# Scores in row groups, all weight splits on VectorE, a planner that knows of a shared port

## Chip, cores and metric

One core of a Trainium2 chip runs the whole program. The metric is the device time of one execution in microseconds (us), lower is better. Before the change three timed runs gave 1037.95, 1039.11 and 1043.07, median 1039.11.

## What is computed

A trunk of two layers on x of 256 positions by 1024 features, all in float32. Each layer is a SwiGLU feed-forward net (FFN), a mixer, and a second FFN, every one between two RMS norms:

```python
for l in range(2):
    h = rmsnorm(x, g[0]);  x = x + 0.5 * rmsnorm(swiglu(h, wg[l,0], wu[l,0], wd[l,0]), g[1])
    h = rmsnorm(x, g[2])
    m = even_mixer(h, ...) if l % 2 == 0 else odd_mixer(h, ...)
    x = x + rmsnorm(m, g[3])
    h = rmsnorm(x, g[4]);  x = x + 0.5 * rmsnorm(swiglu(h, wg[l,1], wu[l,1], wd[l,1]), g[5])
# even mixer, A: 4 heads, two softmaxes each, 64 wide:  w = p0 - lam * p1;  o = rmsnorm(w @ v, subln) * 0.8
# even mixer, B: 8 heads on the 64 keys that an indexer selects:
#     score = sum over 8 indexer heads of relu(qi . ki) * wi   (32 wide),  top-64 of it,  softmax
# odd mixer, C: 16 heads, 64 wide, a band with a relative-position bias
```

`swiglu(h) = (silu(h wg) * (h wu)) wd` with 2816 hidden features.

## The kernel before

**Products.** A float32 product is three TensorE products on rounded halves: hi x hi, lo x hi, hi x lo (`mm3`, L381, lines 383 to 385; `products`, L364, lines 375, 376, 378). Weights come by DMA on SP's queue into a `raw` tile (`Unit.start`, L245). ScalarE casts 512 columns to `wh` (L264), and `wl = raw - wh` follows (L266) on VectorE (DVE) or GpSimd (POOL). Of 664 such splits 33 run on POOL, all in the two mixers: 20 from 191 to 316 us and 13 from 709 to 820 us. Activations are split likewise when a PSUM bank is emptied (`split`, L346: hi by ScalarE in L351, lo by DVE in L357).

**Stages.** First FFN 0 to 190 us, even mixer to 340, two FFNs to 708, odd mixer to 840, last FFN. A norm ends a stage and begins the next: `postnorm` (L467) updates X (L487), `prenorm` (L418) squares, takes a root on POOL (`rstd`, L409, lines 411 to 415), multiplies by g (L430 or L440), transposes on TensorE (L393) and splits into `xTh`, `xTl`. Matmuls of the other half of the positions fill in.

**Attention.** `split_keys` (L658) writes the transposed keys into KB with one head of a pair in partitions 0 to 63 and the other in 64 to 127, each in its own columns, with zeros elsewhere (`zeros`, L315), in two ScalarE and two DVE instructions of 64 partitions. `scores` (L685) then does two heads at once in six 128-row matmuls with 256 (first 128 queries) or 512 columns. It is called 16 times: 4 A heads, 4 B pairs, 8 C pairs. `soft` (L701) adds the mask, takes the maximum and the exponential. An A head divides its first softmax by its sum (L865), scales the second's reciprocal by -lam (L861) and adds it (L869). `select` (L793) computes the indexer's scores: for each of two query tiles and four groups of 32 partitions six matmuls into a bank of its own, a relu, two DVE accumulations.

**Order.** Nothing is ordered by hand. `Plan.op` (L61) records each operation with its engines, a cost, its reads and writes and a due place; `Plan.issue` (L93) is a list scheduler that plays the program through with these costs (and `LAT`, L30, from the end of one to the start of a dependent one) and writes each engine's instructions in the order in which it started them. An engine on the chip keeps this order. A weight split of a mixer may go to POOL where DVE is late by more than `OVER` (L38). The few lines that do it:

```python
if fits and e != o["eng"][0] and eng[o["eng"][0]] < now + o["over"]:
    fits = False                                        # L133, the second engine waits its turn
...
op(DVE if pl.over is None else ("DVE", "POOL"), {"DVE": n_dve(self.step), "POOL": 0.11 + self.step * 0.00218}, lo, ...)
```

Of the kernel before, what the change touches and what calls it, by code (L numbers as in the profile page):

```python
# [9 lines left out]
F32 = mybir.dt.float32  # L10
# [27 lines left out]

OVER = (None, 0.45, 0.5)
# [13 lines left out]
class Plan:  # L53
# [39 lines left out]
    def issue(self):  # L93
# [3 lines left out]
        ev, n = [], 0  # L97
# [16 lines left out]
        while ev:  # L114
# [7 lines left out]
            for e in heap:  # L122
# [3 lines left out]
                while heap[e]:  # L126
# [6 lines left out]
                    if fits and e != o["eng"][0] and eng[o["eng"][0]] < now + o["over"]:  # L133
                        fits = False
# [17 lines left out]
                us = o["us"][e] if isinstance(o["us"], dict) else o["us"]  # L152
                o["fn"](e) if isinstance(o["us"], dict) else o["fn"]()
                end = eng[e] = o["end"] = now + us
# [28 lines left out]
def trunk_kernel(  # L183
# [52 lines left out]
    class Unit:  # L236
# [8 lines left out]
        def start(self, n):  # L245
# [13 lines left out]
            for i, p in enumerate(range(0, f, self.step)):  # L259
# [5 lines left out]
                def lo(e, sl=sl):  # L265
                    (nc.vector if e == "DVE" else nc.gpsimd).tensor_sub(  # L266
                        ref.t[1][:, sl], raw.t[:, sl], ref.t[0][:, sl].bitcast(F32))
                op(ACT, n_act(self.step), hi, r=[rk], w=[(ref, i, 0)], pos=q)
                op(DVE if pl.over is None else ("DVE", "POOL"), {"DVE": n_dve(self.step), "POOL": 0.11 + self.step * 0.00218}, lo,
                   r=[rk, (ref, i, 0)], w=[(ref, i, 1)], pos=q + 0.05)  # L270
# [42 lines left out]
    KB.t = tuple(cp.tile([P, 4, 2 * S], F32R, name="KB" + c) for c in "hl")  # L313

    def zeros():  # L315
        for z in KB.t:
            nc.gpsimd.memset(z[0:64, :, S:2 * S].bitcast(F32), 0.0)
            nc.gpsimd.memset(z[64:P, :, 0:S].bitcast(F32), 0.0)
# [19 lines left out]
    def more_consts(after):  # L338
# [3 lines left out]
        op(POOL, 3.6, zeros, w=[(KB, "z")], after=after, pos=60.0)  # L342
# [3 lines left out]
    def split(dst, wk, src, rk, n, scale=None, sk=(), psum=True, pos=None):  # L346
# [14 lines left out]
        op(ACT, n_act(n, psum, int(callable(scale))), hi, r=list(rk) + list(sk), w=wk[0], pos=pos)  # L361
        op(DVE, n_dve(n), lo, r=list(rk) + list(sk) + wk[0], w=wk[1], pos=pos)
# [46 lines left out]
    def rstd(s, ep, pos):  # L409
# [3 lines left out]
        op(POOL, 0.11, lambda: nc.gpsimd.tensor_add(s.t[:, 2:3], s.t[:, 2:3], s.t[:, 1:2]), r=[(s, 1)], w=[(s, 2)], pos=pos)  # L413
        def power():
            nc.gpsimd.tensor_tensor(s.t[:, 3:4], s.t[:, 2:3], nhalf.t[:, 0:1], op=ALU.pow)
        op(POOL, 0.46, power, r=[(s, 2), nhalf], w=[(s, 3)], pos=pos)

    def prenorm(t, xT, g):  # L418
# [48 lines left out]
    def postnorm(t, y, g, half, final):  # L467
# [16 lines left out]
        for h, c0, n in CUTS if final else [(h, 0, 512) for h in range(2)]:  # L484
# [4 lines left out]
            o = op(DVE, n_dve(n) + 0.06, up, r=[yg[h], (s, 3)], w=[(X[t], h)], pos=pos)  # L489
# [584 lines left out]
```

## Time and profile before

| | |
|---|---|
| runs | 1037.95, 1039.11, 1043.07 us |
| the profiled execution | 1040.63 us, span 1038.9, mean granted clock 0.995 |
| PE busy | 1012.1 us, 97% of the span |
| DVE, ACT, POOL busy | 664.6 (64%), 555.1 (53%), 94.6 (9%) |
| DMA | 185.46 MB, 179 GB/s |

The times of all views come from the one profiled execution. Its own time of 1040.63 us holds the span of 1038.9 and 1.7 us around it. Matmuls overlap in the trace (a 512-column matmul is shown as 0.39 us, and one starts every 0.23 us), so PE's cost is read from start to start. An idle time in brackets names the engine, tile and line that ended it.

### The profile page before, as it was taken

The page shows a single profiled execution, that of the slowest core. Times are in us where ns is not written, and L with a number is a line of the kernel's source. Part 1 is how long each engine was busy: PE and PEld are TensorE (multiplying, and loading weights), DVE is VectorE, ACT ScalarE, POOL GpSimd, SP SyncE. Part 2 cuts the span into 40 slices and gives each one's busy share as a digit, 9 for nine tenths or more (in the row PEclk, how much of TensorE's full clock was granted, in tenths as well). Part 3 has the DMA queues.
Part 4 walks back from the last instruction along what each step waited for, and adds up shares of the span by engine and source line. Part 5 has one row for each costly group of instructions (what it writes and reads, how often), then busy time and mean ns, then how long its engine had stood idle before and what let it go on. Part 6 is the DMA issues. An engine that isn't in the chain of part 4 may idle for free.

```text
span 1038.9 us, 14338 instructions
## 1 busy us (share of the span) xinstructions
PE 1012.1 (97%) x5070; PEld 850.1 (82%) x5070; DVE 664.6 (64%) x1278; ACT 555.1 (53%) x1142; POOL 94.6 (9%) x117
## 2 busy tenths in 40 slices
PE   8999999999999999999999999999989999999997
PEld 7888888776778988888888888887889888888886
DVE  6655555689998765555487545555677886555552
ACT  7544444555657654454366544544567766444541
POOL 2000000232431100000010000003121110000000
PEclk9999999999999999999999999998999999999999
DMA  8866665463244576665457656654594356656641
GB/s 267 289 184 183 196 186 166 136 213 104 83 162 124 175 255 190 188 184 194 150 203 229 194 183 184 191 194 120 173 278 145 118 164 205 199 183 184 190 133 41
DMA packets 94152, 185.46 MB, mean 179 GB/s; under 512 B 7040, under 2 KB 29440, under 8 KB 94080
## 3 DMA queue, kind: packets, MB, share of 16 engines
q1 hardware_dynamic: 94080, 184.54, 56.8%
q8 instruction: 40, 0.66, 0.3%
q14 instruction: 32, 0.26, 0.1%
HBM read 183.47 MB, written 1.05 MB: 178 GB/s over the span
## 4 chain that ended last, share of the span: by engine, by line
PE 83%; DVE 8%; DMA 4%; issue 2%; ACT 2%; POOL 1%; SPq 0%; POOLq 0%; DVEq 0%; ACTq 0%
PE ps L384 14%; PE ps L383 14%; PE ps L385 14%; PE y L383 9%; PE y L384 9%; PE y L385 9%; PE ps L393 4%; PE ps L375 3%; PE ps L376 3%; PE ps L378 3%; DVE wl L266 2%; ACT wh L264 1%; DMA raw<-in_ow_in_dram 1%; DMA raw<-in_wg_dram 1%; DMA raw<-in_wu_dram 1%
## 5 line engine op out<-in xcount | busy, mean ns | idle before, releaser
L266 DVE TENSOR_TENSOR wl<-raw,wh 128x512 fp32r<-128x512 f32 x631 | 421.4, 708 | 286.0 <-ACT wh L264 285.2
L264 ACT CAST wh<-raw 128x512 fp32r<-128x512 f32 (+1 forms) x664 | 378.1, 616 | 319.1 <-PE ps L385 173.4
L384 PE MATMUL ps<-wl,xTh 128*128 128x512 f32 x592 | 231.0, 390 | 0.0
L383 PE MATMUL ps<-wh,xTh 128*128 128x512 f32 x592 | 231.0, 390 | 0.0
L385 PE MATMUL ps<-wh,xTl 128*128 128x512 f32 x592 | 230.9, 390 | 0.0
L383 PE MATMUL y<-wh,blk 128*128 128x512 f32 x352 | 140.2, 398 | 0.0
L385 PE MATMUL y<-wh,blk 128*128 128x512 f32 x352 | 138.2, 393 | 0.0
L384 PE MATMUL y<-wl,blk 128*128 128x512 f32 x352 | 137.9, 392 | 0.0
L385 PEld LDWEIGHTS ps<-wh,xTl 128*128 128x128 f32 x592 | 111.5, 188 | 23.3
L383 PEld LDWEIGHTS ps<-wh,xTh 128*128 128x128 f32 x592 | 111.5, 188 | 23.2
L384 PEld LDWEIGHTS ps<-wl,xTh 128*128 128x128 f32 x592 | 111.4, 188 | 23.0
L375 PE MATMUL ps<-wh,xTh 128*128 128x512 f32 (+2 forms) x320 | 108.4, 354 | 0.9 <-ACT xTh L351 0.9
L376 PE MATMUL ps<-wl,xTh 128*128 128x512 f32 (+2 forms) x320 | 105.6, 346 | 0.2 <-DVE wl L266 0.2
L413 POOL TENSOR_TENSOR sm<-sm 128x1 f32<-128x1 f32 x24 | 9.8, 408 | 767.2 <-ACT t L476 714.9
L385 PEld LDWEIGHTS y<-wh,blk 128*128 128x128 f32 x352 | 66.6, 189 | 14.3
L383 PEld LDWEIGHTS y<-wh,blk 128*128 128x128 f32 x352 | 66.8, 190 | 13.2
L384 PEld LDWEIGHTS y<-wl,blk 128*128 128x128 f32 x352 | 66.8, 190 | 13.2
L393 PE MATMUL ps<-ident,t 128*128 128x128 f32 x386 | 58.8, 278 | 13.3 <-DVE t L546 2.9
L393 PEld LDWEIGHTS ps<-ident,t 128*128 128x128 f32 x386 | 44.6, 141 | 29.5 <-issue 5.9
L375 PEld LDWEIGHTS ps<-wh,xTh 128*128 128x128 f32 x320 | 61.0, 191 | 7.8 <-ACT xTh L351 1.1
L376 PEld LDWEIGHTS ps<-wl,xTh 128*128 128x128 f32 x320 | 60.9, 190 | 6.7 <-DVE wl L266 0.6
L378 PE MATMUL ps<-wh,xTl 128*128 128x512 f32 (+2 forms) x320 | 65.8, 344 | 0.0
(129 smaller groups left out, 1071.8 us busy)
## 6 DMA issues: line engine op xcount, KB each, us to landing
raw<-in_wu_dram SPq DMA_DIRECT2D x88, 512.0 KB, 4.3
raw<-in_wd_dram SPq DMA_DIRECT2D x88, 512.0 KB, 3.5
raw<-in_wg_dram SPq DMA_DIRECT2D x86, 512.0 KB, 3.7
raw<-in_ew_in_dram SPq DMA_DIRECT2D x24, 512.0 KB, 3.8
raw<-in_ow_in_dram SPq DMA_DIRECT2D x24, 512.0 KB, 4.8
g<-in_norm_g_dram SPq DMA_DIRECT2D x11, 512.0 KB, 5.3
raw<-in_ew_out_dram SPq DMA_DIRECT2D x8, 512.0 KB, 3.9
raw<-in_ow_out_dram SPq DMA_DIRECT2D x8, 512.0 KB, 3.6
```

What stands on the lines that cost most here:

```text
L264: nc.scalar.copy(ref.t[0][:, sl], raw.t[:, sl])
L266: (nc.vector if e == "DVE" else nc.gpsimd).tensor_sub(ref.t[1][:, sl], raw.t[:, sl], ref.t[0][:, sl].bitcast(F32))
L375: nc.tensor.matmul(o(), ah, bh, start=k == 0, stop=False)
L376: nc.tensor.matmul(o(), ah, bl, start=False, stop=False)
L378: nc.tensor.matmul(o(), al, bh, start=False, stop=k == KT - 1)
L383: nc.tensor.matmul(o, ah, bh, start=start, stop=False)
L384: nc.tensor.matmul(o, ah, bl, start=False, stop=False)
L385: nc.tensor.matmul(o, al, bh, start=False, stop=stop)
L393: nc.tensor.transpose(b.t[:, k * P:(k + 1) * P], s[:, k * P:(k + 1) * P], ident.t)
L413: op(POOL, 0.11, lambda: nc.gpsimd.tensor_add(s.t[:, 2:3], s.t[:, 2:3], s.t[:, 1:2]), r=[(s, 1)], w=[(s, 2)], pos=pos)
```

## The change

1. POOL does no weight split: all 664 are DVE's. `OVER` is gone.
2. The planner has a `port` flag: POOL's operations and DVE's with two inputs in SBUF play one after another. An operation for PE is ready `SAFE` = 0.6 us later than before. ScalarE's latency is 0.14 instead of 0.07, POOL's small operations of a norm cost 0.27 and 0.52 instead of 0.11 and 0.46, and a few others more.
3. KB has no zeros: its columns are halved, `split_keys` is one ScalarE and one DVE instruction of 128 partitions, and `zeros` is gone. `scores` gives each head a bank, and does twelve matmuls of 64-row groups, the two groups in turn.
4. `select` takes four banks at once and does its 24 matmuls of a query tile round the four 32-row groups in turn, in one visit for each tile.
5. The first softmax of an A head is not divided: the second is scaled by -lam r0/r1, and the squared sum r0² goes into the epsilon of the norm that follows.

```diff
-LAT = {"PE": 0.2, "ACT": 0.07, "DVE": 0.13, "POOL": 0.17, "DMA": 2.0}
+LAT = {"PE": 0.2, "ACT": 0.14, "DVE": 0.13, "POOL": 0.17, "DMA": 2.0}
+SAFE = 0.6
-OVER = (None, 0.45, 0.5)
...
-                end = eng[e] = o["end"] = now + us
+                start = now
+                if o["port"]:
+                    start = max(start, port)
+                    port = start + us
+                end = eng[e] = o["end"] = start + us
...
-                    d["ready"] = max(d["ready"], end + (OWN[e] if d["eng"] == (e,) else o["lat"]))
+                    d["ready"] = max(d["ready"], end + (OWN[e] if d["eng"] == (e,) else o["lat"] + (SAFE if d["eng"] == ("PE",) else 0.0)))
...
-                op(DVE if pl.over is None else ("DVE", "POOL"), {"DVE": n_dve(self.step), "POOL": 0.11 + self.step * 0.00218}, lo,
+                op(DVE, n_dve(self.step), lo, r=[rk, (ref, i, 0)], w=[(ref, i, 1)], pos=q + 0.05, port=True)
...
-    KB.t = tuple(cp.tile([P, 4, 2 * S], F32R, name="KB" + c) for c in "hl")
+    KB.t = tuple(cp.tile([P, 4, S], F32R, name="KB" + c) for c in "hl")
...
-        for r in range(2):
-            rs = slice(64 * r, 64 * r + 64)
-            split(lambda rs=rs, r=r: tuple(z[rs, b0:b0 + n, r * S + c0:r * S + c0 + w] for z in KB.t),
+        split(lambda: tuple(z[:, b0:b0 + n, c0:c0 + w] for z in KB.t),
...
             def f(t=t):
-                mm3(bs[t].t[:, 0:2 * KL[t]].rearrange("p (h c) -> p h c", h=2), tuple(z[:, bq, t * P:(t + 1) * P] for z in q()),
-                    tuple(z[:, bk, :].rearrange("p (h c) -> p h c", h=2)[:, :, 0:KL[t]] for z in KB.t), True, True)
-            op(PE, 0.327 * (t + 1), f, r=qk + kb_keys(bk), w=[bs[t]], pos=pos, after=after)
+                for i, j in ((0, 0), (0, 1), (1, 0)):
+                    for h in range(2):
+                        rs = slice(64 * h, 64 * h + 64)
+                        nc.tensor.matmul(bs[h].t[:, QS[t]], q()[i][rs, bq, t * P:(t + 1) * P], KB.t[j][rs, bk, 0:KL[t]],
+                                         start=i + j == 0, stop=i == 1)
+            op(PE, 0.36, f, r=qk + kb_keys(bk), w=[(b, t) for b in bs], pos=pos, after=after)
...
+            for i in range(2):
+                def f(i=i):
+                    for x, z in ((0, 0), (0, 1), (1, 0)):
+                        for g in range(4):
+                            rs = slice(32 * g, 32 * g + 32)
+                            nc.tensor.matmul(bs[g].t[:, i * kl:(i + 1) * kl], iT.v()[x][rs, i, t * P:(t + 1) * P],
+                                             iT.v()[z][rs, 2, 0:kl], start=x + z == 0, stop=x == 1)
+                op(PE, 0.36, f, r=ik, w=[(b, i) for b in bs])
...
-                nc.vector.reciprocal(ri.t, r.t)
-                nc.vector.tensor_scalar(ri.t[:, 2:4], ri.t[:, 2:4], nlam.t, None, op0=ALU.mult)
+                nc.vector.reciprocal(ri.t[:, 2:4], r.t[:, 2:4])
+                nc.vector.scalar_tensor_tensor(ri.t[:, 2:4], ri.t[:, 2:4], nlam.t, r.t[:, 0:2], op0=ALU.mult, op1=ALU.mult)
+                nc.vector.tensor_mul(rsq.t[:, :, h], r.t[:, 0:2], r.t[:, 0:2])
...
-                def nr(t=t, e=es[0], ri=ri):
-                    nc.vector.tensor_scalar(e.t[:, QS[t]], e.t[:, QS[t]], ri.t[:, t:t + 1], None, op0=ALU.mult)
```

**Where the order moves.** In the rows below a number behind a name counts the tiles, so the same tile has another number in the two kernels; the line of a matmul is 5 less in the changed kernel.

First place: PE's queue at the start, where the second half of x is transposed (`t_50`) between the first gate and up matmuls of the first FFN. Before:

```order
L383 MATMUL ps_380<-wh_261,xTh_130 128x512
L384 MATMUL ps_380<-wl_262,xTh_130 128x512
L385 MATMUL ps_380<-wh_261,xTl_131 128x512
L393 MATMUL ps_386<-ident,t_50_378 128x128 x2
L383 MATMUL ps_373<-wh_261,xTh_130 128x512
L384 MATMUL ps_373<-wl_262,xTh_130 128x512
```

And with the change:

```order
L378 MATMUL ps_376<-wh_259,xTh_131 128x512
L379 MATMUL ps_376<-wl_260,xTh_131 128x512
L380 MATMUL ps_376<-wh_259,xTl_132 128x512
L388 MATMUL ps_393<-ident,t_50_373 128x128 x2
L378 MATMUL ps_369<-wh_284,xTh_131 128x512
L379 MATMUL ps_369<-wl_285,xTh_131 128x512
```

The transposes stand behind 12 matmuls of the weight tile where they stood behind 6.

Second place: PE's queue where the second FFN pair ends (`y`, the down product) and the odd mixer begins (`xTh`, the normed and transposed x). Before:

```order
L385 MATMUL y_5382<-wh_6316,blk_6394 128x512
L393 MATMUL ps_6528<-ident,t_1180_6479 128x128 x4
L393 MATMUL ps_6536<-ident,t_1183_6491 128x128 x4
L383 MATMUL y_5377<-wh_6336,blk_6393 128x512
...
L385 MATMUL y_5382<-wh_6377,blk_6394 128x512
L375 MATMUL ps_6584<-wh_6468,xTh_6542 128x512
```

And with the change:

```order
L380 MATMUL y_5408<-wh_6389,blk_6430 128x512
L388 MATMUL ps_6572<-ident,t_1182_6517 128x128 x4
L388 MATMUL ps_6579<-ident,t_1183_6523 128x128 x4
L378 MATMUL y_5414<-wh_6389,blk_6430 128x512
...
L380 MATMUL y_5414<-wh_6410,blk_6431 128x512
L370 MATMUL ps_6612<-wh_6501,xTh_6588 128x512
```

Behind the eight transposes stood 18 matmuls of the down product (the "..." holds 16 of them), now 9 (7): the transposes come 9 matmuls later.

Third place: PE's queue at the first pair of the odd mixer's scores. `ps_6946` is the next Q projection. Before:

```order
L385 MATMUL ps_6946<-xTh_6542,wl_6777 128x256
L383 MATMUL ps_6990<-KBh,blk_6872 128x256
L384 MATMUL ps_6990<-KBl,blk_6872 128x256
L385 MATMUL ps_6990<-KBh,blk_6872 128x256
L383 MATMUL ps_6995<-KBh,blk_6872 128x512
L384 MATMUL ps_6995<-KBl,blk_6872 128x512
```

And with the change:

```order
L688 MATMUL ps_7016<-KBh,blk_6905 128x128
L688 MATMUL ps_7017<-KBh,blk_6905 128x128
L688 MATMUL ps_7016<-KBl,blk_6905 128x128
L688 MATMUL ps_7017<-KBl,blk_6905 128x128
...
L688 MATMUL ps_7016<-KBh,blk_6905 128x256
L688 MATMUL ps_7017<-KBh,blk_6905 128x256
```

Six matmuls are twelve with half the columns each, in two banks by turns; they stand behind as many Q matmuls as before.

## Rows read from the trace of the kernel before

**Rows 1.** The profile page's first part, the span's busy time, share and instructions by engine.

```profile
PE 1012.1 (97%) x5070; PEld 850.1 (82%) x5070; DVE 664.6 (64%) x1278; ACT 555.1 (53%) x1142; POOL 94.6 (9%) x117
```

**Rows 2.** Table by stretch: us of the span, its length, busy us (and instructions) of PE, PEld, DVE, ACT, POOL, granted clock, DMA share, GB/s. Four stretches of the even mixer, the boundary to the odd mixer, one stretch inside the odd mixer.

```profile
208.00:234.00 26.00, 25.42 (x133) 20.28 (x132) 23.26 (x46) 14.46 (x28) 10.49 (x12) 1.00 0.64 214
234.00:260.00 26.00, 23.86 (x118) 17.97 (x118) 24.31 (x65) 14.72 (x37) 6.73 (x5) 1.00 0.33 100
260.00:286.00 26.00, 23.89 (x130) 19.79 (x129) 25.83 (x82) 15.78 (x47) 11.60 (x8) 1.00 0.28 84
286.00:312.00 26.00, 23.86 (x118) 18.62 (x117) 23.95 (x55) 14.28 (x40) 9.52 (x8) 1.00 0.47 160
702.00:728.00 26.00, 23.42 (x94) 18.79 (x93) 16.16 (x24) 13.65 (x30) 8.78 (x10) 0.87 0.41 122
780.00:806.00 26.00, 26.00 (x204) 24.94 (x203) 21.06 (x65) 19.35 (x52) 5.38 (x7) 1.00 0.49 148
```

**Rows 3.** Groups of instructions from 208 to 312 us, DVE's and then POOL's: count, busy us, mean ns of one, idle before and what ended it.

```profile
L266 DVE TENSOR_TENSOR wl<-raw,wh 128x512 fp32r<-128x512 f32 x33 | 32.7, 1031 | 1.4 <-ACT wh L264 1.3
L357 DVE TENSOR_TENSOR KBl<-ps,KBh 64x512 fp32r<-64x512 f32 x8 | 5.5, 688 | 1.7 <-ACT KBh L351 1.6
L865 DVE TENSOR_SCALAR t<-t,sm 128x256 f32<-128x256 f32 x4 | 1.4, 348 | 0.0
L865 DVE TENSOR_SCALAR t<-t,sm 128x128 f32<-128x128 f32 x4 | 1.1, 277 | 0.0
L861 DVE TENSOR_SCALAR sm<-sm,nlam 128x2 f32<-128x2 f32 x4 | 0.9, 230 | 0.1
...
L266 POOL TENSOR_TENSOR wl<-raw,wh 128x512 fp32r<-128x512 f32 x15 | 21.5, 1449 | 33.7 <-ACT wh L264 33.7
L642 POOL TENSOR_TENSOR t<-t,t 128x512 f32<-128x512 f32 x8 | 11.8, 1469 | 14.5 <-DVE t L639 14.5
```

**Rows 4.** DVE's timeline: one weight split in the even mixer, four in the odd one where POOL does no large work. Start, us, engine, line, operation, count, idle before.

```profile
246.41 1.77 DVE L266 TENSOR_TENSOR wl<-raw,wh 128x512 fp32r<-128x512 f32 x1
...
742.13 2.50 DVE L266 TENSOR_TENSOR wl<-raw,wh 128x512 fp32r<-128x512 f32 x4 [3.55 <-ACT wh L264]
```

**Rows 5.** PE's timeline at the start of the program, the transposes of `t_50` and a matmul behind them.

```profile
23.50 0.39 PE L385 MATMUL ps<-wh,xTl 128*128 128x512 f32 x1
26.31 0.44 PE L393 MATMUL ps<-ident,t 128*128 128x128 f32 x2 [2.43 <-DVE t L546]
...
28.00 0.63 PE L385 MATMUL ps<-wh,xTl 128*128 128x512 f32 x1
```

**Rows 6.** The boundary to the even mixer: PE's transposes, DVE's product with g, POOL's weight splits.

```profile
194.28 0.66 PE L393 MATMUL ps<-ident,t 128*128 128x128 f32 x4 [0.87 <-DVE t L430]
195.50 0.66 PE L393 MATMUL ps<-ident,t 128*128 128x128 f32 x4 [0.56 <-DVE sm L411]
...
192.93 2.52 DVE L430 TENSOR_TENSOR t<-X,g 128x512 f32<-128x512 f32 x2
...
191.25 3.65 POOL L266 TENSOR_TENSOR wl<-raw,wh 128x296 fp32r<-128x296 f32 x3 [0.27 <-ACT wh L264]
```

**Rows 7.** The boundary to the odd mixer: DVE's scaling by the root and g (the first half of the positions, and the second, 18 us later), PE's transposes, two of the matmuls behind them.

```profile
714.19 3.43 DVE L440 SCALAR_TENSOR_TENSOR t<-X,sm,g 128x512 f32<-128x512 f32 x2 [0.44 <-POOL sm L415]
732.31 1.40 DVE L440 SCALAR_TENSOR_TENSOR t<-X,sm,g 128x512 f32<-128x512 f32 x2
...
716.00 0.66 PE L393 MATMUL ps<-ident,t 128*128 128x128 f32 x4 [1.56 <-DVE t L440]
717.67 1.11 PE L393 MATMUL ps<-ident,t 128*128 128x128 f32 x4 [1.02 <-DVE t L440]
719.44 0.63 PE L385 MATMUL y<-wh,blk 128*128 128x512 f32 x1
723.28 0.62 PE L385 MATMUL y<-wh,blk 128*128 128x512 f32 x1
```

**Rows 8.** The first scores of the odd mixer: PE's two waits, and ScalarE's casts of the keys.

```profile
764.33 0.38 PE L383 MATMUL ps<-KBh,blk 128*128 128x256 f32 x1 [1.47 <-ACT KBh L351]
765.75 0.38 PE L384 MATMUL ps<-KBl,blk 128*128 128x256 f32 x1 [1.04 <-DVE KBl L357]
...
763.11 1.17 ACT L351 CAST KBh<-ps 64x512 fp32r<-64x512 f32 x2
```

**Rows 9.** One of `select`'s eight visits with 32-row matmuls on PE, and the 128-row matmuls before and behind it.

```profile
243.00 0.40 PE L376 MATMUL ps<-wl,xTh 128*128 128x512 f32 x1
243.32 0.38 PE L383 MATMUL ps<-blk 32*128 32x256 f32 x1
243.55 0.28 PE L384 MATMUL ps<-blk,blk 32*128 32x256 f32 x1
...
244.02 0.28 PE L385 MATMUL ps<-blk,blk 32*128 32x256 f32 x1
244.23 0.50 PE L375 MATMUL ps<-wh,xTh 128*128 128x512 f32 x1
244.56 0.40 PE L376 MATMUL ps<-wl,xTh 128*128 128x512 f32 x1
```

**Rows 10.** A call of `scores` where PE does not wait: its three matmuls of 512 columns, and the next matmul.

```profile
318.71 0.40 PE L383 MATMUL ps<-KBh,blk 128*128 128x512 f32 x1
...
319.41 0.40 PE L383 MATMUL y<-wh,xTh 128*128 128x512 f32 x1
```

More of the change, by code (lines that the diff above doesn't have):

```diff
@@ L96, in issue @@
         heap = {e: [] for e in LAT}
-        ev, n = [], 0
+        ev, n, port = [], 0, 0.0
         todo = len(self.ops)
@@ L341, in more_consts, with split @@
         op(POOL, 0.7, mask, w=[cmask], after=after, pos=60.0)
-        op(POOL, 3.6, zeros, w=[(KB, "z")], after=after, pos=60.0)
         op(POOL, 0.2, lambda: nc.gpsimd.tensor_scalar(sub8.t, subc.t, 1.0 - LAM0, None, op0=ALU.mult), r=[subc], w=[sub8], pos=60.0)
-    def split(dst, wk, src, rk, n, scale=None, sk=(), psum=True, pos=None):
+    def split(dst, wk, src, rk, n, scale=None, sk=(), psum=True, pos=None, more=0.0):
         def hi():
@@ L430, in mg @@
                     nc.vector.tensor_mul(xn[h].t, X[t].t[:, HS[h]], g.t[:, HS[h]])
-                op(DVE, n_dve(512), mg, r=[(X[t], h), (g, h)], w=[xn[h]], pos=pos - 0.01)
+                op(DVE, n_dve(512), mg, r=[(X[t], h), (g, h)], w=[xn[h]], pos=pos - 0.01, port=True)
             q = t2() if late else xn[h]
@@ L488, in up @@
                                                op0=ALU.mult, op1=ALU.add)
-            o = op(DVE, n_dve(n) + 0.06, up, r=[yg[h], (s, 3)], w=[(X[t], h)], pos=pos)
+            o = op(DVE, n_dve(n) + 0.06, up, r=[yg[h], (s, 3)], w=[(X[t], h)], pos=pos, port=True)
             if final:
@@ L734, in nr @@
                 nc.vector.tensor_scalar(e.t[:, QS[t]], e.t[:, QS[t]], ri.t[:, t:t + 1], None, op0=ALU.mult)
-            op(DVE, n_dve(KL[t], True) + 0.06, nr, r=[ri], w=[(e, t)], pos=pos)
+            op(DVE, n_dve(KL[t], True) + 0.06, nr, r=[ri], w=[(e, t)], pos=pos, port=True)
         tr = transp_p(e, z, hh, pos)
@@ L760, in src @@
                 return s.rearrange("p (t c) -> p t c", c=P) if rev else s
-            split(dst, ([(oT, bi, hh, 0)], [(oT, bi, hh, 1)]), src, [(ob, 0), (ob, 1)], S, pos=pos)
+            split(dst, ([(oT, bi, hh, 0)], [(oT, bi, hh, 1)]), src, [(ob, 0), (ob, 1)], S, pos=pos, more=0.1)
     def ok(oT, bi):
@@ L810, in acc @@
                                                        cmask.t[:, sl] if z else sc[0].t[:, sl], op0=ALU.mult, op1=ALU.add)
-                    op(DVE, n_dve(kl) + 0.06, acc, r=[rl, wI[t], cmask], w=[(sc[0], t)])
+                    op(DVE, n_dve(kl) + 0.06, acc, r=[rl, wI[t], cmask], w=[(sc[0], t)], port=True)
             m8 = const([P, 8], f"m8_{t}")
@@ L869, in ad @@
                                                    e[0].t[:, QS[t]], op0=ALU.mult, op1=ALU.add)
-                op(DVE, n_dve(KL[t]) + 0.06, ad, r=[ri, (es[1], t)], w=[(es[0], t)], pos=pos)
+                op(DVE, n_dve(KL[t]) + 0.06, ad, r=[ri, (es[1], t)], w=[(es[0], t)], pos=pos, port=True)
             z = new_pt(1)
@@ L1016, in nxt @@
                     prenorm(t, z, gn)
-            pl.over = OVER[0 if p != 1 else 1 + l]
             if p == 1:
```

67 lines of the change are left out of this document (28 added, 39 removed).

## The prediction

> **What bounds the kernel now.** First the busy shares: PE works 97% of the span, the next engine 64% [rows 1]. So time is to be had only where PE waits, runs at half clock, or spends matmul time that the change removes. PE idles 1038.9 - 1012.1 = 26.8 us. The table by stretch says where the mixers stand [rows 2]: in the even mixer, 208 to 312 us, PE is busy 97.03 of 104 us, a quarter of all its idle time, and DVE 97.35: there DVE is as full as PE, though over the whole span it idles a third. In the odd mixer (780 to 806 us) PE is busy for all of 26.00 us with DVE at 21.06. The stretch from 702 to 728 us shows a granted clock of 0.87 and PE at 23.42.
>
> The groups of the even mixer tell what fills DVE [rows 3]: 33 weight splits at 1031 ns. The same split takes 0.6 to 0.7 us where POOL does no large work: four in 2.50 us at 742, against one of 1.77 us at 246 [rows 4]. POOL has 15 splits at 1449 ns and eight rope additions at 1469 ns in the stretch, and DVE is slower while they run.
>
> **The change, part by part.** Every term is against the profiled execution's own 1040.6 us; the median of the runs is 1.5 us below it.
>
> *Start.* PE waits 2.43 us for `t_50` (start to start 23.50 to 26.31) and then shows half clock, 0.63 us a matmul [rows 5]. With the change six more matmuls stand ahead of the transposes. Six at 0.23 us each fill 1.4 us of the wait. Their weights (`wh`, `wl` of the same tile) are the same that the next rows used, so nothing new is waited for. Bounds: 0 if the weights are late, and 4.2 if the whole wait goes and the clock does not fall. I take **-1.4**.
>
> *Boundary to the even mixer.* PE waits 0.87 and 0.56 us for DVE, and each four transposes at 0.66 us take about 0.16 more than the usual pitch [rows 6]. DVE's two products with g take 2.52 us, 1.26 each, against 0.70 for a DVE instruction of that size at 732.31 [rows 7]; three splits on POOL run beside them, from 191.25 to 194.90. Without these DVE is some 1.1 us earlier, less one split of 296 columns that now stands ahead (estimated at 296/512 of 0.65, 0.4); and the planner's 0.6 us puts six matmuls in front of the transposes. I take the whole, 0.87 + 0.56 + 2 x 0.16 = **-1.7**; the other end is -0.5.
>
> *Even mixer, 208 to 312 us.* DVE sets the pace, so its work counts. Against it: 15 splits come over from POOL, 15 x 0.60 = +9.0 us. For it: (a) the 33 splits lose what POOL costs them, 33 x (1.031 - 0.69) = 11.3 us, of which the splits' share of POOL's large work is 21.5 / (21.5 + 11.8 + 2.0 for two smaller additions) = 0.61, so -6.9; (b) the eight L865 instructions go, -2.5; (c) four key splits of eight go, as 128 partitions take as long as 64, 4 x 0.69 = -2.8; (d) the new scaling has three small instructions in place of two, each 0.2: +0.8. The sum is -2.4 us for DVE. It does not count DVE's other instructions that POOL held up, whose part I can't separate. On the other side DVE's own idle time is 104 - 97.35 = 6.65 us, and PE's 6.97, which the planner's margin and the whole visits may in part fill: -2.4 - 6.65 = -9. I take **-6**, near the middle, since both ends rest on sums with parts left out. `select` now takes four banks at once, and the A heads' output needs two of these later; a late relu would hold them back, which the +-3 holds.
>
> PE has less to do in `select` there. A visit now costs (243.00 to 244.56, less two matmuls of 0.23) 1.10 us, of which six matmuls of 0.118 are 0.71 and the change of row size 0.39 [rows 9]; eight are 8.8 us. Two visits of 24 are 2 x (24 x 0.118 + 0.39) = 6.4 if the loads of four groups stay one behind the other, 2.2 if all four run side by side. I count nothing for it: DVE covers it in this stretch. If DVE is no longer the bound, it is worth up to 6.6 more.
>
> The rows show DVE paying for part of POOL's time: a split takes 1031 ns in the mean beside POOL's work, and 1.77 at the worst [rows 3, 4]. The Trainium skill, page "SBUF — State Buffer", on the shared port pair, says that a two-input DVE instruction and a GpSimd instruction that reads SBUF exclude each other, the second one waiting in full. By that rule DVE would gain all of POOL's split time and this term would be rival (c)'s, and the mean of 1031 ns agrees with it only in part.
>
> *Boundary to the odd mixer.* PE waits 1.56 and 1.02 us for L440, which takes 3.43 us for two (1.40 for two at 732) [rows 7], and then shows half clock: from 719.44 to 723.28 nine matmuls start 0.43 us apart, not 0.23. POOL's splits no longer run beside L440, and nine down-product matmuls (2.1 us) stand ahead of the transposes that stood behind. The waits and the first slow four are 1.56 + 1.02 + 0.16 = 2.7 us; from 717.67 to 719.44 four transposes and two matmuls take 1.77 where 0.44 + 0.46 would do, 0.9 more; and nine matmuls at 0.2 give 1.8. I take **-5.4**, all of it; the other end is -1.5, if only POOL's part goes.
>
> *First scores of the odd mixer.* PE waits 1.47 us for ScalarE's second key cast and 1.04 for DVE's second key split [rows 8]. Now each is one instruction: 0.58 us less on ScalarE (half of 1.17), 0.69 less on DVE [rows 3]. The casts of weights ahead of it on ScalarE wait for a DMA as before. I take **-1.3**, the ends being 0 and -2.5.
>
> *Scores.* A call takes three 512-column matmuls in 0.70 us, and three of 256 at half of it: 1.05 [rows 10]. With the change it has twelve matmuls, each with weights of its own. A matmul with 32 rows, its own weights and 256 columns starts every 0.118 us [rows 9], so the twelve take between 12 x 0.06 (the two row groups side by side) and 12 x 0.118, plus 0.37 for the change of row size twice. I take the lower end, as PE's loads already run beside its matmuls (850.1 us of loads within the span) [rows 1]: 1.09 us, +0.04 a call; with three calls cut in two by other matmuls the 12 calls (4 B and 8 C pairs) in stretches where PE sets the pace give **+0.6**.
>
> The Trainium skill, page "TensorE: Matmul & The Clock Gate", Part 3 on packing, says that tiles in different row groups run at the same time; "TensorEngine Tiling (Array Packing)", Key Properties, says that changing the tiling mode drains the engine while changing the tile does not. The 0.39 us in row 9's visit agrees with the second; no run here yet shows the first.
>
> *The rest.* No DMA is added, removed or moved past another. The removed zeros (POOL, in the first FFN), the other key splits and one square on DVE lie beside PE work of the FFN or of the odd mixer, where DVE has 5 us of 26 to spare [rows 2]. If that cover goes, the odd mixer's four key splits are 2.8 us less and its 13 splits from POOL 7.8 us more.
>
> Sum: -1.4 - 1.7 - 6 - 5.4 - 1.3 + 0.6 = -15.2, 1040.6 to **1025.4** by own time, so 1023.9 for a median like that of before. I put the prediction at **1024**.
>
> **The rivals.** *(a) Row groups one behind the other.* If the two groups' loads and matmuls run in turn, a call is 12 x 0.113 + 0.37 = 1.73 us, +0.7 over before, 12 calls +8: about 1033. For it: no row shows two groups at work at once; against: loads overlap everywhere else. *(b) The even mixer gains nothing.* DVE pays 9 us for POOL's work, is relieved by little, and the terms cancel; -6 becomes 0: about 1031. For it: DVE has 97.35 of 104 us already. (a) and (b) together: about 1039, no change. *(c) More waits go.* If every us of a POOL split held up DVE, the even term is 9.0 - 21.5 = -12.5, 6.5 more than taken; the start's wait and half clock may go whole (2.8 more); 1023.9 - 9.3 = 1014.6, and with DVE no longer the bound some 2 of `select`'s 6.6 us come on top: about 1012. The page named above states such a lock. For it: the 1.77 us split beside POOL; against: the mean of 1031 ns. *(d) Slower.* Each alternation of row group costs PE like the change of row size itself does, some 0.1 us added to every matmul: a call is 12 x 0.2 + 0.37 = 2.8 us, +1.75 for each of 12 calls is +21, and `select` loses 2 x 24 x 0.1 = 5 where DVE covers only part: about 1048. It decides from 0.185 us per matmul on, a call of 2.6 us. Against it: six 32-row matmuls in one group start 0.118 us apart. *(e) The planner's margin does nothing*: the transposes are placed later but DVE is later by as much; both boundary terms, -7.1, shrink to -2: about 1029, within the forecast's own range.
>
> **How the numbers follow.** The forecast with its own range 1016 to 1031: 0.47. (a) alone 0.18, (b) alone 0.11, both 0.10, (c) 0.08, (d) 0.06. A measurement of this kernel tells about half a per cent, 5.2 us, from no change. Faster by more: 0.46 of the forecast, 0.14 of (a), 0.09 of (b), 0.08 of (c): 0.77. Slower: all of (d) and 0.01 of both: 0.07. The rest, 0.16, is within. The range 1012 to 1036 holds the forecast, (a), (b) and half of (c), and leaves out both together, (d) and the rest of (c), about 0.2.
>
> **What would show it.** In the changed profile: weight splits on DVE near 0.65 us in the even mixer and none on POOL; PE's waits for L430 and L440's successors at the two boundaries under 0.3 us, and a granted clock near 1.00 from 702 to 728 us; one key cast of 128 partitions of about 0.6 us; a score call of about 1.1 us from the matmul before it to the one behind it, its twelve matmuls some 0.06 apart, and `select`'s visits under 2 us. Wrong it would be if score matmuls start 0.11 us or more apart, if DVE in the even mixer is still full and PE waits as long as before, or if new waits for DVE appear where splits used to be POOL's, in the odd mixer above all.

## The result and the profile after

The changed kernel takes 1024.89 us (median of 4 runs, 1023.56 to 1026.63), against 1038.6 in the same runs of the kernel before: a ratio of 0.9853, interval 0.9835 to 0.9872. (Ratios here are formed from the fast runs of a session and are not the quotient of two medians, which would be 0.9868.) 1024 was predicted. The profiled execution took 1024.73 us, with a span of 1022.3.

The parts, from the first to the last instruction, by the starts of the first and the last down-product matmul (`y<-wh,blk`, `y<-wl,blk`) of each of the four FFNs:

| us | start to 1st down | 1st down | even mixer | 2nd, 3rd FFN to 3rd down | 3rd down, boundary | odd mixer | 4th down | end |
|---|---|---|---|---|---|---|---|---|
| before | 48.6 | 154.0 | 176.6 | 187.6 | 158.1 | 155.3 | 152.2 | 6.4 |
| after | 46.1 | 152.1 | 170.6 | 187.1 | 152.3 | 156.6 | 151.2 | 6.5 |
| difference | -2.5 | -1.9 | -6.0 | -0.5 | -5.9 | +1.3 | -1.0 | 0 |

("Even mixer" goes from the last down product of the first FFN to the first of the second, so the second FFN's gate is in it; "odd mixer" likewise. "1st down" holds the first norm boundary.)

First the page's busy shares [rows 1]: POOL's time halves, DVE's is 7 us less although it took 33 splits over.

```profile
PE 1000.7 (98%) x5166; PEld 845.3 (83%) x5166; DVE 657.3 (64%) x1299; ACT 548.1 (54%) x1134; POOL 43.7 (4%) x80
```

The two boundaries and the start on PE's and DVE's timelines, columns as in [rows 5 to 7]:

```profile
26.59 0.40 PE L380 MATMUL ps<-wh,xTl 128*128 128x512 f32 x1
26.82 0.38 PE L388 MATMUL ps<-ident,t 128*128 128x128 f32 x2
26.96 0.47 PE L378 MATMUL ps<-wh,xTh 128*128 128x512 f32 x1
...
190.37 1.28 DVE L425 TENSOR_TENSOR t<-X,g 128x512 f32<-128x512 f32 x2
192.07 1.03 PE L388 MATMUL ps<-ident,t 128*128 128x128 f32 x8
...
703.07 1.41 DVE L435 SCALAR_TENSOR_TENSOR t<-X,sm,g 128x512 f32<-128x512 f32 x2
705.14 0.40 PE L380 MATMUL y<-wh,blk 128*128 128x512 f32 x1
705.38 1.03 PE L388 MATMUL ps<-ident,t 128*128 128x128 f32 x8
```

At these three places no transpose waits any more, eight stand in one visit of 1.03 us at the boundaries, and DVE's pair takes 1.28 and 1.41 us where it took 2.52 and 3.43 [rows 6, 7].

The even mixer's stretches [rows 2] and its groups [rows 3], here from 200 to 312 us:

```profile
208.00:234.00 26.00, 25.29 (x169) 20.94 (x169) 22.98 (x44) 15.64 (x32) 6.40 (x7) 1.00 0.56 190
234.00:260.00 26.00, 24.11 (x142) 19.02 (x141) 25.47 (x88) 16.22 (x44) 1.29 (x1) 1.00 0.27 83
260.00:286.00 26.00, 25.59 (x141) 21.09 (x140) 25.76 (x68) 15.93 (x47) 7.17 (x6) 1.00 0.46 161
286.00:312.00 26.00, 26.00 (x161) 21.07 (x159) 25.18 (x83) 18.36 (x50) 0.00 (x0) 1.00 0.52 157
312.00:338.00 26.00, 21.71 (x122) 18.34 (x119) 24.05 (x55) 17.78 (x46) 3.78 (x6) 0.93 0.58 177
...
L269 DVE TENSOR_TENSOR wl<-raw,wh 128x512 fp32r<-128x512 f32 x62 | 40.2, 682 | 1.2 <-ACT wh L267 1.1
```

A split takes 682 ns where it took 1031. From 208 to 312 us PE is busy 100.99 of 104 us, was 97.03; but from 312 to 338 only 21.71 of 26. Over the whole part of the table ("even mixer"), before and after:

```profile
202.60:379.20 176.60, 169.63 (x904) 139.44 (x903) 156.04 (x375) 109.78 (x265) 46.78 (x43) 1.00 0.50 159
198.20:368.80 170.60, 163.29 (x953) 136.02 (x952) 150.13 (x387) 107.79 (x264) 21.41 (x26) 0.99 0.52 170
```

PE's idle time is 6.97 us before and 7.31 after, and DVE's 20.56 and 20.47: neither has shrunk, PE's has moved to the end of the part. What is some 6 us less is the work, PE's (169.63 to 163.29) and DVE's (156.04 to 150.13) alike.

A call of `scores` (twelve 64-row matmuls) and a visit of `select` (24 of 32 rows) with their neighbours on PE:

```profile
240.30 0.39 PE L371 MATMUL ps<-wl,xTh 128*128 128x512 f32 x1
240.62 0.33 PE L688 MATMUL ps<-KBh,blk 64*128 64x128 f32 x2
240.79 0.28 PE L688 MATMUL ps<-KBl,blk 64*128 64x128 f32 x2
240.90 0.44 PE L688 MATMUL ps<-KBh,blk 64*128 64x128 f32 x4
241.18 0.28 PE L688 MATMUL ps<-KBl,blk 64*128 64x256 f32 x2
241.30 0.28 PE L688 MATMUL ps<-KBh,blk 64*128 64x256 f32 x2
241.51 0.50 PE L370 MATMUL ps<-wh,xTh 128*128 128x512 f32 x1
241.84 0.40 PE L371 MATMUL ps<-wl,xTh 128*128 128x512 f32 x1
...
224.84 0.33 PE L801 MATMUL y<-blk 32*128 32x128 f32 x4
225.01 0.39 PE L801 MATMUL y<-blk,blk 32*128 32x128 f32 x8
225.23 0.28 PE L801 MATMUL y<-blk 32*128 32x128 f32 x4
225.34 0.39 PE L801 MATMUL y<-blk,blk 32*128 32x128 f32 x8
225.67 0.50 PE L370 MATMUL ps<-wh,xTh 128*128 128x512 f32 x1
```

The "x2" is the news: two matmuls in different row groups start mostly 3 or 4 ns apart, and the next pair 0.11 us later, with 128 or 256 columns alike. From 240.30 to 241.84, less two 512-column matmuls of 0.23, the call costs 1.08 us. Four groups of `select` start together in the same way; its two visits cost 1.02 and 1.06 us, where eight cost about 1.10 each [rows 9].

Last the places where PE waits now: the end of the even mixer, the first scores of the odd mixer, the end of the odd mixer, and the clock of two stretches.

```profile
328.30 0.39 PE L380 MATMUL y<-wh,xTl 128*128 128x512 f32 x1
329.79 1.23 PE L388 MATMUL ps<-ident,t 128*128 128x128 f32 x8 [1.11 <-DVE t L425]
332.45 0.39 PE L370 MATMUL ps<-wh,xTh 128*128 128x256 f32 x1 [1.43 <-ACT xTh L346]
...
747.12 0.33 PE L688 MATMUL ps<-KBh,blk 64*128 64x128 f32 x2 [1.03 <-ACT KBh L346]
747.97 0.33 PE L688 MATMUL ps<-KBl,blk 64*128 64x128 f32 x2 [0.52 <-DVE KBl L352]
...
827.23 1.23 PE L388 MATMUL ps<-ident,t 128*128 128x128 f32 x8 [1.16 <-DVE t L425]
829.89 0.39 PE L370 MATMUL ps<-wh,xTh 128*128 128x256 f32 x1 [1.43 <-ACT xTh L346]
...
332.00:336.00 4.00, 3.55 (x18) 3.55 (x19) 3.68 (x8) 0.89 (x2) 1.47 (x4) 0.61 0.57 148
750.00:753.00 3.00, 3.00 (x17) 3.00 (x17) 2.65 (x10) 2.25 (x8) 0.31 (x1) 0.55 1.06 315
```

In the kernel before, six matmuls of the even mixer's output product stood behind its last transposes, and nothing waited there; at the end of the odd mixer only the gate's first matmul did:

```profile
342.11 1.03 PE L393 MATMUL ps<-ident,t 128*128 128x128 f32 x8
342.90 0.48 PE L383 MATMUL y<-wh,xTh 128*128 128x512 f32 x1
...
843.49 1.04 PE L393 MATMUL ps<-ident,t 128*128 128x128 f32 x8
845.43 0.38 PE L375 MATMUL ps<-wh,xTh 128*128 128x256 f32 x1 [0.90 <-ACT xTh L351]
```

### The profile page after: what moved, and what is told of

The parts are those of the page before. It is cut to its first block, busy times and chain, and to the rows that moved or that the text cites. A ratio compares the mean times of both kernels' runs of the same rounds, so it can differ in the third digit from the quotient of the medians.

```text
span 1022.3 us, 14425 instructions
## 1 busy us (share of the span) xinstructions
PE 1000.7 (98%) x5166; PEld 845.3 (83%) x5166; DVE 657.3 (64%) x1299; ACT 548.1 (54%) x1134; POOL 43.7 (4%) x80
## 3 DMA queue, kind: packets, MB, share of 16 engines
HBM read 183.47 MB, written 1.05 MB: 180 GB/s over the span
## 4 chain that ended last, share of the span: by engine, by line
PE 93%; DVE 3%; ACT 2%; DMA 1%; issue 1%; SPq 0%; POOLq 0%; DVEq 0%; POOL 0%; ACTq 0%
PE ps L378 14%; PE ps L379 14%; PE ps L380 14%; PE y L378 9%; PE y L380 9%; PE y L379 9%; PE ps L370 6%; PE ps L371 5%; PE ps L373 5%; PE ps L388 4%; PE ps L688 1%; DVE wl L269 1%; DMA raw<-in_ow_in_dram 1%; ACT wh L267 1%; DMA raw<-in_wg_dram 0%
## 5 line engine op out<-in xcount | busy, mean ns | idle before, releaser
L269 DVE TENSOR_TENSOR wl<-raw,wh 128x512 fp32r<-128x512 f32 (+1 forms) x664 | 427.6, 684 | 273.2 <-ACT wh L267 272.1
L380 PEld LDWEIGHTS ps<-wh,xTl 128*128 128x128 f32 x592 | 111.1, 188 | 23.1
L370 PE MATMUL ps<-wh,xTh 128*128 128x512 f32 (+2 forms) x320 | 110.6, 360 | 4.5 <-ACT xTh L346 3.1
L371 PE MATMUL ps<-wl,xTh 128*128 128x512 f32 (+2 forms) x320 | 107.8, 351 | 0.0
L370 PEld LDWEIGHTS ps<-wh,xTh 128*128 128x128 f32 x320 | 62.8, 196 | 12.5 <-ACT xTh L346 3.9
L388 PE MATMUL ps<-ident,t 128*128 128x128 f32 x386 | 55.9, 273 | 5.7 <-DVE t L425 2.3
L373 PEld LDWEIGHTS ps<-wh,xTl 128*128 128x128 f32 x320 | 52.1, 193 | 6.7
```

What stands on the lines that cost most here:

```text
L269: nc.vector.tensor_sub(ref.t[1][:, sl], raw.t[:, sl], ref.t[0][:, sl].bitcast(F32))
L370: nc.tensor.matmul(o(), ah, bh, start=k == 0, stop=False)
L371: nc.tensor.matmul(o(), ah, bl, start=False, stop=False)
L373: nc.tensor.matmul(o(), al, bh, start=False, stop=k == KT - 1)
L380: nc.tensor.matmul(o, al, bh, start=False, stop=stop)
L388: nc.tensor.transpose(b.t[:, k * P:(k + 1) * P], s[:, k * P:(k + 1) * P], ident.t)
```

## The experiments

Theory 1: POOL's weight splits cost DVE more than they save, above all at the norms, so their absence is the main gain; the planner's margin earns the start and some of the boundaries; the row groups earn PE nothing. Rival: the planner's new rules make the gain. Every edit changes the planner's list, so the order moves in many places. The ratio is to the kernel before in the same session; x 1039 us it is read as us; a difference of two ratios and one of two medians can lie 3 us apart. Times of parts are those of the one profiled execution, which took 2.8 us less than the median of its runs in e2 and e3, and 3.6 to 4.3 more in e6, e7 and e8.

| | edit | median us | ratio, interval |
|---|---|---|---|
| changed | | 1024.89 | 0.9853, 0.9835 to 0.9872 |
| e1 | changed, splits on POOL again | 1033.54 | 0.9941, 0.9924 to 0.9958 |
| e2 | changed, margin 0 | 1025.09 | 0.9873, 0.9845 to 0.9900 |
| e3 | changed, old keys and scores | 1026.68 | 0.9889, 0.9862 to 0.9915 |
| e4 | changed, no port rule | 1018.71 | 0.9813, 0.9792 to 0.9833 |
| e5 | before, no splits on POOL | 1033.18 | 0.9927, 0.9906 to 0.9948 |
| e6 | before, margin 0.6 | 1036.18 | 0.9976, 0.9953 to 0.9999 |
| e7 | changed, first softmax divided | 1025.14 | 0.9847, 0.9824 to 0.9870 |
| e8 | changed, old select | 1026.36 | 0.9863, 0.9830 to 0.9895 |
| e9 | e4 with margin 0 | 1021.26 | 0.9809, 0.9784 to 0.9835 |
| e10 | e4 with margin 0.3 | 1024.90 | 0.9849, 0.9816 to 0.9882 |
| e11 | changed, port rule on large work only | 1020.43 | 0.9806, 0.9778 to 0.9834 |
| e12 | e4 with old keys and scores | 1024.05 | 0.9861, 0.9836 to 0.9887 |

**e1.** In the planner and in `Unit.start` the choice of the engine is put back (the lines of the planner are left out here):

```diff
-                op(DVE, n_dve(self.step), lo, r=[rk, (ref, i, 0)], w=[(ref, i, 1)], pos=q + 0.05, port=True)
+                op(DVE if pl.over is None else ("DVE", "POOL"), {"DVE": n_dve(self.step), "POOL": 0.11 + self.step * 0.00218}, lo,
+                   r=[rk, (ref, i, 0)], w=[(ref, i, 1)], pos=q + 0.05, port=True)
```

> The changed kernel, with the mixers' weight splits allowed on GpSimd again (same thresholds as before; the port flag on them). Theory 1, that POOL's splits cost DVE more than they save it: the mean split on DVE in the even mixer goes back from 0.68 to about 1.0 us, the even mixer (last down product of FFN 1 to the first of FFN 2) gets 4 to 8 us longer than its 170.6, the stretch with the odd boundary 2 to 5 longer than its 152.3; 8 to 13 us in all, 1033 to 1038. Rival, that the planner's margin and port rule made the gain: under 3 us in all, since the planner now knows of the port and puts splits on POOL only where it sees room.

The ratio is 0.0088 up, 9 us, with the intervals apart. But with its other costs the planner now gives POOL 54 splits where the kernel before has 33 (37 for 20 up to the even mixer, 17 for 13 from the odd boundary on), so this is more than the step back. The odd boundary and the odd mixer together take 314.1 us (308.9 in the changed kernel), the even mixer 173.5 (170.6). The stretch with the odd boundary alone is not longer, 151.2 us for 152.3: all of the down product now stands ahead of the transposes, and the cost falls into the odd mixer, 163.0 us for 156.6. At the odd boundary, on DVE, POOL and PE:

```profile
709.01 3.46 DVE L440 SCALAR_TENSOR_TENSOR t<-X,sm,g 128x512 f32<-128x512 f32 x2 [0.44 <-POOL sm L415]
...
708.94 6.33 POOL L272 TENSOR_TENSOR wl<-raw,wh 128x512 fp32r<-128x512 f32 x4
...
713.44 0.50 PE L375 MATMUL ps<-wh,xTh 128*128 128x512 f32 x1 [1.94 <-ACT xTh L351]
715.18 0.63 PE L375 MATMUL ps<-wh,xTh 128*128 128x512 f32 x1
```

Four splits on POOL cover L440's 3.46 us: DVE's half of the old picture [rows 7], in spite of margin and port rule. PE waits 1.94 us and then runs at half clock; but this wait is for a cast of ScalarE, which stood behind two weight casts and a square there until 712.81 us, with no down product left to cover it. So slow splits and a changed order both have a part in it, and e1 doesn't tell them apart. At the first boundary POOL slows DVE as well (L430's pair takes 1.92 us for 1.28), and no transpose waits: the first down takes 152.4 us. The sum falls to theory 1, but the even mixer's share (+2.9, not 4 to 8) and the stretch with the boundary don't.

**e2.** `-SAFE = 0.6`, `+SAFE = 0.0`.

> The changed kernel with SAFE = 0. Theory 1 (the margin earns the two boundaries and the start): waits for the transposes come back at the boundaries, +0.5 to +1.5 at the first, +1 to +3 at the odd one, +1 to +2 at the start; 3 to 6 us in all, 1028 to 1031. Rival (POOL's absence alone makes DVE early enough): within 1.5 us of the changed kernel.

The intervals overlap, and the profile has the first down at 152.2 us, the boundary at 152.5 and the start at 45.4. So the margin earns neither boundary nor start: this part of theory 1 falls. At the end of the odd mixer it even costs. There e2 has three matmuls of the output product behind each four transposes, and neither these nor the next gate wait:

```profile
824.90 0.60 PE L388 MATMUL ps<-ident,t 128*128 128x128 f32 x4
826.02 0.60 PE L388 MATMUL ps<-ident,t 128*128 128x128 f32 x4
827.15 0.28 PE L370 MATMUL ps<-wh,xTh 128*128 128x256 f32 x1
```

The changed kernel has no product left at this place and waits 1.16 + 1.43 us. e2's odd mixer takes 153.6 us for 156.6. The same holds for the other runs: with a margin of 0.6 all nine kernels here wait for these transposes (0.82 to 1.16 us) and for the gate (1.13 to 1.44); with none, e2 and e9 wait for neither, and the kernel before and e5 for the gate alone (0.90 and 0.91).

**e3.** The old `split_keys`, `zeros` and `mm3` scores in the changed kernel.

```diff
-                for i, j in ((0, 0), (0, 1), (1, 0)):
-                    for h in range(2):
-                        rs = slice(64 * h, 64 * h + 64)
...
+                mm3(bs[t].t[:, 0:2 * KL[t]].rearrange("p (h c) -> p h c", h=2), tuple(z[:, bq, t * P:(t + 1) * P] for z in q()),
+                    tuple(z[:, bk, :].rearrange("p (h c) -> p h c", h=2)[:, :, 0:KL[t]] for z in KB.t), True, True)
```

> The changed kernel with the old keys (zeros, two splits of 64 partitions) and six 128-row matmuls a call; one slot less for small tiles, 15 for 16, as the memory is full. Theory 1 (a call costs 1.06 against 1.09 us, so the row groups earn nothing on PE, and only the merged key split counts): even mixer +1 to +3 for 2.8 us of DVE, first scores of the odd mixer +0.5 to +1.5, the rest -0.3; +1 to +4 in all. Rival (the row groups earn PE time): +5 or more, with PE's busy time in the odd mixer up by over 2 us.

The edit also has 15 slots for small tiles in place of 16. 0.0036 up, 3.7 us, with the intervals just overlapping; by the medians it is 1.8. The even mixer takes 171.7 us (170.6), the odd one 154.9 (156.6). PE's busy time is 999.0 us against 1000.7: not less with row groups.

**e4.** `"port": port or eng == ("POOL",)` becomes `"port": False`.

> The changed kernel, whose planner takes no operation for one on the shared port. Theory 1 (with the splits gone from POOL its large work is ten rope additions, 13 us, so the rule has little left to say): within 2 us of the changed kernel, all of it in the even mixer. Rival (the rule made the even mixer's gain): the even mixer 3 to 6 us longer.

A miss for both: 4 us faster than the changed kernel by the ratios, intervals just apart, and 6 by the medians. The even mixer takes 166.9 us, the start 44.5, the odd mixer 154.9. Of the even mixer's 3.7 us, 1.7 are waits of PE (5.60 us for 7.31), and about as much is the half clock at its end, which e4 does not show. Over the whole kernel, by the granted clocks of the runs (0.994 to 0.997, in the changed kernel 0.991 to 0.994), some 3 of the 6 us are half clock. The rule, or the order it made, cost time.

**e5.** In the kernel before, `OVER = (None, None, None)`.

> The kernel before with one edit: no weight split on GpSimd (OVER is None for all stages), its planner as it was. Theory 1, now that the changed kernel with SAFE = 0 kept both boundaries: POOL's absence alone makes DVE early there. Last down stretch of the third FFN (29.2 us before, 23.3 with the change) down to 23.5 to 26, that of the first FFN (25.25, 23.33) to 23.5 to 24.5, even mixer (176.6) to 171 to 175; 7 to 13 us in all, 1027 to 1033. Rival (the planner's rules are needed, since DVE now takes 33 splits more): within 4 us of before.

The one edit gives 0.9927, 7.6 us, about half of the whole. The first down takes 152.2 us and the boundary 152.8, with the kernel before's own planner:

```profile
711.20 1.41 DVE L440 SCALAR_TENSOR_TENSOR t<-X,sm,g 128x512 f32<-128x512 f32 x2 [0.44 <-POOL sm L415]
...
711.56 0.39 PE L385 MATMUL y<-wh,blk 128*128 128x512 f32 x1
712.00 1.32 PE L393 MATMUL ps<-ident,t 128*128 128x128 f32 x8
```

L440 stands behind three splits on DVE as before and takes 1.41 us for 3.43; the transposes wait 0.05, with 18 matmuls of the down product behind them as before, so it is not their place that moved. But the even mixer takes 177.6 us, 1.0 more than before.

**e6.** In the kernel before, the 0.6 us for PE's operations.

> The kernel before with one edit: SAFE = 0.6 in its planner, splits on GpSimd as before. Theory 1: the start gains 1.5 to 3, the boundaries keep most of their slow DVE: third FFN's last down stretch 26 to 29 us; 2 to 5 us in all. Rival (the margin makes the boundaries): that stretch under 25 and 8 us or more in all.

2.5 us by the ratio, with an interval that nearly holds no change. Start 45.3, boundary 156.1: in these executions the margin alone takes 2.1 of the boundary's 5.9 us, and POOL's absence 5.3 alone.

**e7 and e8.** L865 (the division) put back with the old scaling and the plain `EPS`; `select` with a bank and six matmuls for each group, eight visits.

> The changed kernel with the A heads' first softmax divided again (eight instructions, 2.5 us on DVE; 0.8 for the new scaling goes). Theory 1 (DVE sets the pace in the even mixer): the even mixer 1 to 2.5 us longer, nothing else. Rival (PE or the attention's chain sets it, and DVE's work is hidden): within 0.5 us.

> The changed kernel with select's old eight visits (8.6 us of PE in place of 2 x 1.04). If DVE sets the pace in the even mixer throughout, it is hidden: within 1 us. If PE sets it, 4 to 6.5 us longer. Theory 1 takes the first, nearer to 2 us, since PE was busy 25.3 to 26 of 26 us in three of the changed kernel's five stretches there.

e7 is no slower than the changed kernel, e8 by 1.0 us within the intervals. Their profiled executions lie 3.6 us above their medians, so their parts can't be laid beside the others' to the us. No gain of either part is shown in the kernel's time. What e8's execution does show is that the old visits are work of PE again. Its even mixer:

```profile
198.20:372.00 173.80, 168.97 (x953) 139.73 (x952) 149.25 (x385) 107.12 (x263) 22.30 (x26) 0.99 0.51 166
```

PE works 5.7 us more than in the changed kernel and idles 2.5 less (4.83 for 7.31), which makes the part 3.2 us longer.

**e9, e10, e11.** Without the port rule, with a margin of 0 and of 0.3; and with the rule on POOL's operations of over 0.6 us alone.

```diff
-             "port": port or eng == ("POOL",),
+             "port": port or eng == ("POOL",) and us > 0.6,
```

> The changed kernel without the port rule (1018.7) and with SAFE = 0 too. By the stages of the two single runs: the odd mixer loses the margin's 3.0 us (156.6 to 153.6 there), the rest stays; if the two add up, 1015 to 1017. If what each gave was the same waits, or only another draw of the list scheduler's order, 1018 to 1022.

> The changed kernel without the port rule and with SAFE = 0.3. If the margin's size matters by a rule, between e4 (1018.7 at 0.6) and e9. If the order moves by chance with every such number, it may lie outside of both by 1 to 3 us.

> The changed kernel, in whose planner GpSimd's operations under 0.6 us (the norms' small additions and roots) are free of the port; the rope additions keep the rule. If the rule costs by holding the norms' roots behind DVE's queue (start and boundaries), 1020 to 1022, with the even mixer between 167 and 170.6. If it costs by the rope additions in the even mixer, no change there: 1023 to 1025.

e9 and e11 are as fast as e4 by the ratio; e10, between e4 and e9, is as slow as the changed kernel. The intervals of e9 and e10 overlap a little, but in their one session each of e10's four runs (1024.23 us and more) is above each of e9's (1022.30 and less). A margin that makes no difference at 0 and 0.6 makes one of 4 us at 0.3: with such numbers the list scheduler draws another order, and an order is worth some 4 us by itself. In e9 the start took 48.4 us, nearly all the start's gain lost, and the even mixer 166.7.

**e12.** e4 with e3's keys and scores.

> The kernel of e4 (no port rule, margin 0.6, 1018.7) with e3's old keys and 128-row scores (15 slots for small tiles). Theory 1: on PE a call costs the same either way (1.06 and 1.09), and the merged key splits are worth 1 to 3 us, mostly in the even mixer: 1019.5 to 1022. Rival, from e3's odd mixer (154.9 against 156.6): the row groups cost the odd mixer 1.7 us by themselves, so 1016 to 1018.5.

0.0048 up on e4, 5.0 us, the intervals apart by 0.0003, with 3.7 in the even mixer (170.6 for 166.9) and 1.8 at the start (46.3 for 44.5), which has no scores: so another draw of the order is in the sum. The rival of this run, that row groups cost the odd mixer 1.7 us, falls: 154.7 and 154.9.

## Why the prediction came out

The time came out, and so did both boundaries and the scores' price; the working of the even mixer and the odd mixer's term did not, and that the sum met the time so closely is in part luck.

*Odd boundary*, -5.4 predicted, -5.9 measured, by the mechanism named: e5 has 5.3 of it with that one edit. e1 brings the slow L440 and 5.2 us back, but with more splits and partly by a wait of another kind. *First boundary*, -1.7 and -1.9: e5 has it with that edit too (152.2), and e1 doesn't take it back (152.4), so there the changed planner keeps it even with POOL's splits beside it. In both the prediction also gave a part to the planner's placing of the transposes; e2 and e5 show that none is needed. So rival (e) had a true premise, that the margin does nothing there, and a wrong price: both terms stayed.

*Start*, -1.4 and -2.5: the whole wait of 2.43 us and the half clock behind it went, as at the term's far end, and part of it came back at the first weights: waits of 0.41 and 0.70 us, and a granted clock of 0.50 from 9 to 15 us, where the kernel before has 1.00. In the runs here this part is anything from 44.5 to 48.4 us, with and without the margin. The step that gave it to six more matmuls in front of the transposes isn't confirmed.

*Scores*, +0.04 a call predicted, +0.03 measured (1.08 for 1.05). Two row groups run side by side (a pair of 256 columns each in 0.11 us, where one took 0.118 [rows 9]), so rivals (a) and (d) fall. That this still gains nothing has the reason the sum gave: twelve matmuls with weights of their own in six pairs of 0.11 us are 0.7, and the change of row size is nearly 0.4 a visit. What the rows after show of the Trainium skill's "TensorE: Matmul & The Clock Gate", Part 3 on packing, agrees with it: different row groups start mostly 3 or 4 ns apart.

*Even mixer*, -6 predicted, -6.0 measured, and the parts behind it were not these. (1) The step that failed is "DVE sets the pace": it took the idle time of DVE and PE to be filled in part, and counted nothing for `select`. In the stretch it looked at, 208 to 312 us, PE's idle time fell from 6.97 to 3.01 us, but came back behind it: over the part neither idle time shrank, the work did. On PE, `select`'s two visits of 1.02 and 1.06 us stand for eight of 1.10, 6.7 us less. On DVE the work fell by 5.9 us, where the sum had -2.4 for the stretch it looked at. How much of the 6 us belongs to which engine is open: e8 gives `select` 3.2 us in this part of its one profiled execution, and 1.0 us of the kernel's time, which is within the intervals. (2) "POOL's splits on DVE +9.0, relief -6.9" said +2.1, with 0.60 us for a split that comes over, where its own rows have 0.625 and the changed kernel 0.682; at 0.682 it would be +3.3. e5 has +1.0, which agrees in sign, but an order alone moves this part by more (3.7, e4). (3) It gave -2.5 to the A heads' division; e7 shows no gain. (4) It gave -2.8 to the merged keys; with the row groups e12 has 3.7 there and e3 1.1, right in sign, with the size open. (5) It had nothing for the order that the port rule makes, which is 3.7 us longer here than e4's. Errors in both directions met at -6: this is luck. Which of the rest stands for what is open: put back, and more of them (e1), the POOL splits cost 2.9 us in this part; taken from the kernel before by themselves (e5) they gave nothing.

The end of this part was not foreseen either. PE begins the output product 14.6 us earlier, counted from the first FFN's last down product (110.1 us before, 95.5 after), and 8.6 of this is gone by the next FFN's down product. The product's matmuls are done before the norm's transposes, so none is left to cover them, and PE waits 1.11 and 1.43 us and then shows a granted clock of 0.61 for 4 us. How much of the 14.6 was a gain and how much only an earlier place was not tried.

*First scores and odd mixer*, -1.3 and most of the scores' +0.6 predicted, +1.3 measured: the other step that failed. The wait is 1.03 + 0.52 us for 1.47 + 1.04, so 0.96 less, as priced. The prediction priced no follow-up, and there are two. After these waits PE shows a granted clock of 0.55 from 750 to 753 us, nearly all of it at the lower level (1.2 GHz; 256-column matmuls 0.21 us apart for 0.12), where the kernel before has 1.00 from 767 to 770 us after its longer waits; and the odd mixer's last transposes and the next gate wait 1.16 and 1.43 us, where only the gate waited in the kernel before, 0.90 us. Each is worth about 1.7 us. Neither is a price of the row groups: e5, with the keys and scores of before, also shows half clock behind its waits of 1.15 and 1.04 us (0.50 from 758.5 to 761.5) and takes 156.5 us; and the waits at the end go with the margin (e2). "New waits for DVE in the odd mixer" was the prediction's own sign of being wrong, and it appeared; but e2 has the same splits on DVE and not this wait, so it isn't theirs.

The last FFN's -1.0 was in no term.

Of the cases, the forecast itself came true. Rival (b), that the even mixer gains nothing, holds for POOL's splits alone (e5) and not for the change. (By their own sums (a) would be about 1031.5 and (b) 1029.9, each about 1 us under what is written; no verdict hangs on it.) What the Trainium skill's "SBUF — State Buffer" says on the shared port pair, that an instruction waits in full, agrees with the boundary: L440's pair is 2.0 us longer beside POOL (3.46 in e1, 1.41 after). Over the even mixer it is not worth what it would make of the sum, -12.5.

The fastest kernels here are e4, e9 and e11, at 0.9806 to 0.9813 with intervals that lie on each other, some 4 us under the changed kernel by the ratios: without its port rule, or with it on POOL's large work alone. That the rule itself is at fault is not shown, since e10 lacks it too and gains nothing.

## What to carry to other kernels

Before work is moved to a second engine to relieve a full one, read what one instruction of the full engine takes with the second at work and without: the splits on POOL looked free, and took most of a boundary (5.3 of 5.9 us, e5). Where two small matmuls are packed into row groups, count the change of row size per visit and the weight load per pair; at this size they eat the gain, and fewer, longer visits are what saves the engine's time (`select`: two of about 1.04 us for eight of 1.10). Whether the kernel gets such a saving is another question: look whether the engine's idle time grows by as much (e8: nearly half). A margin that lets filling work start ahead of a wait leaves none to stand behind it, so look at both sides of each wait (the end of the odd mixer). And where a list scheduler writes the order, any number moves it: a verdict on one of its rules needs several draws, as 4 us came and went with a margin of 0, 0.3 and 0.6.

## What the runs showed of the hardware

Pairs of 64-row matmuls were paced at 0.11 us whether they had 128 or 256 columns, so a pair of the smaller ones costs as much as one of the larger. Four 32-row groups of 128 columns were paced at 0.10 to 0.11 us for the four. And the granted clock fell after waits of 1.03 and 0.52 us (0.55 from 750 to 753) where it did not after 1.47 and 1.04 in the kernel before: the length of the last wait alone does not tell.
